# A hybrid attention and state-space layer: two token tiles to a PSUM bank, weights a job ahead, and the orders of TensorE and VectorE written by hand

## The chip, the cores and the metric

The kernel runs on one core of a Trainium2 chip. The core has a matrix engine (TensorE, PE in the profile), a vector engine (VectorE, DVE), an activation engine (ScalarE, ACT), a general engine (GpSimd, POOL) and a synchronisation engine (SyncE, SP). Each takes its own instructions strictly in order and waits at an instruction until its inputs and buffers are ready. SP and ACT also issue DMAs, in the place where these stand in their order. The metric is the device time of one execution in microseconds (us), given as the median of several runs.

## The reference

One layer over 1024 tokens of width 1024, in fp32, cut to what matters here:

```python
h = rmsnorm(x, g_pre)
q, k, v, g_att, z, xbc, dt_raw, merge_logits = split(h @ w_in)
# branch A: 8 heads, two softmax maps of 64 columns each, causal, with a bias by distance
a = softmax(q1 k1 / 8 + bias) - lam * softmax(q2 k2 / 8 + bias)
o = rmsnorm(a @ v, att_subln_g) * (1 - lambda_init) * silu(g_att)
y_att = o @ w_att_proj
# branch B: 8 groups of 4 heads of 64, state 128
xbc = silu(causal_conv4(xbc)); xs, B, C = split(xbc); dt = softplus(dt_raw + dt_bias)
y = chunked_scan(xs, dt, A, B, C) + xs * d_skip
y_ssm = group_rmsnorm(y * silu(z), ssm_norm_g) @ w_ssm_proj
mixed = sigmoid(gate_att) * y_att + sigmoid(gate_ssm) * y_ssm
out = x + rmsnorm(mixed @ w_out, g_post)
```

## The kernel before

Every fp32 operand of a projection is split into a rounded high part (made by ScalarE, helper `split`, L97) and a low part, the difference (VectorE or GpSimd, L98). A product is three matmuls, high x high, high x low and low x high (`mm3`, L153). A projection "step" with transposed output (`proj_T`) is 12 matmuls of 512 columns, half of a bank of 512 tokens; one with tokens on the partitions (`proj_N`) is 24 matmuls of 256 columns for one tile of 128 tokens.

The stages run one after the other:

- Start: x is loaded, scaled to h, transposed by TensorE (`ptx`) and split into hTH and hTL; keys, queries and values of head 0 are projected.
- Attention: for each of 8 heads, 8 blocks of 128 queries (`Block`, named by head and block). A block makes scores `s` on TensorE, adds the bias and takes the maximum on VectorE (`ng`), exponentials with their sums on ScalarE, and combines both maps on VectorE: `rec` (reciprocal of the sums), `nlam`, then `p`. While the next block begins, TensorE transposes `p` (`pta`), and multiplies it by the values (`po`). After four blocks `normed` computes the norm of the four outputs `o`: 11 small instructions (`rsv`, `rsy`, `rst`), then four products with the gate `gg`. Beside the blocks a stream of jobs, taken in steps (`stream.take`), projects keys (`pk`), queries (`pq`), values and gates (`pv`) of the next head, and the merge gates (`pg`).
- Attention projection (`pya`), then the state-space part: for each of 8 groups, convolutions of B, C and x (`pub`, `puc`, `pux`; evictions to `ub`, `bT` and so on, three taps, a tanh) and the gate z (`pz`), as jobs beside the 8 chunks of the group before. A chunk (`Chunk.prepare` and `advance`) loads decay rows by a DMA (`mt<-arow_d`), turns them into decays on ScalarE (L783), multiplies them by the masked product `cbm` on VectorE, and TensorE makes `pd` of it.
- Last group with the first half of the state-space projection (`pye`) beside it, then the rest of that projection (`pys`), the output projection (`pout`) and the final norm.

Accumulators come from three PSUM pools of two buffers each: `psp` (projections), `pss` (scores, and `pd`), `pst` (transposes, `po`, `px`). Weights come through buffers `raw`, three of them, issued on SP.

TensorE's order is the program's (`manual_schedule(engines={PE})`). The orders of the other engines are made by a scheduler, which goes by the program's order, its own estimates, and marks such as `tc.high_priority(offset=AHEAD)` around evictions.

Of the kernel before, what the change touches and what calls it, by code (L numbers as in the profile page):

```python
# [10 lines left out]
F32 = mybir.dt.float32  # L11
# [6 lines left out]
P = 128  # L18
# [28 lines left out]
AHEAD = 2000  # L47
# [27 lines left out]
def tile_hybrid_layer(ctx: ExitStack, tc: tile.TileContext, x, g_pre, w_in, lq1, lk1, lq2, lk2,  # L75
# [56 lines left out]
    def load_cols(w, row0, col0, width, tag, name, off=0, wh=None, wl=None, eng=None):  # L132

        if wh is None:
            wh = wts.tile([P, KT, width], F32R, tag=tag + "h", name=name + "h")
            wl = wts.tile([P, KT, width], F32R, tag=tag + "l", name=name + "l")
        for c in range(0, width - off, P):
            n = min(P, width - off - c)
            cols = slice(off + c, off + c + n)
            for k0 in range(0, KT, 4):  # L140
                raw = wts.tile([P, 4, P], F32, tag="raw", bufs=3, name=f"{name}r{off + c}_{k0}")
                r0 = row0 + k0 * P
                nc.sync.dma_start(raw[:, :, 0:n], w[r0:r0 + 4 * P, col0 + c:col0 + c + n].rearrange("(k p) c -> p k c", p=P))
                split(wh[:, k0:k0 + 4, cols], wl[:, k0:k0 + 4, cols], raw[:, :, 0:n], eng)
        return wh, wl
# [25 lines left out]
    def proj_N(w, t, n, name):  # L171

        wh, wl = w
        ps = psp.tile([P, 512], F32, tag="pp", name=name)
        sl = slice(t * P, (t + 1) * P)
        mm3(ps[:, 0:n], [((hTH[:, k, sl], hTL[:, k, sl]), (wh[:, k, 0:n], wl[:, k, 0:n])) for k in range(KT)])
        return ps

    class Stream:
# [5 lines left out]
        def add(self, load, steps):  # L185
            self.jobs.append([load, steps, None])

        def load(self, i):
            if i < len(self.jobs) and self.jobs[i][2] is None:
                self.jobs[i][2] = self.jobs[i][0]()  # L190

        def advance(self):

            if self.at is None:
                for i in range(self.ahead + 1):
                    self.load(self.done + i)
                self.at = self.jobs[self.done][1](self.jobs[self.done][2])
            try:
                next(self.at)
                return True  # L200
# [50 lines left out]
    pe_scope.enter_context(tc.manual_schedule(engines={mybir.EngineType.PE}))  # L251
# [10 lines left out]
    class Head:  # L262
# [15 lines left out]
        def keys(self, w, half):  # L278
# [3 lines left out]
            with tc.high_priority(offset=AHEAD):  # L282
                nc.scalar.activation(kh[lo, 0, sl], ps[lo], AF.Copy)
                nc.scalar.activation(kh[hi, 1, sl], ps[hi], AF.Copy)
                nc.vector.tensor_tensor(kl[lo, 0, sl], ps[lo], f32(kh[lo, 0, sl]), op=ALU.subtract)
                nc.vector.tensor_tensor(kl[hi, 1, sl], ps[hi], f32(kh[hi, 1, sl]), op=ALU.subtract)
            for part in (kh, kl):
                nc.scalar.dma_start(f32(part[hi, 0, sl]), f32(part[lo, 0, sl]))
                nc.scalar.dma_start(f32(part[lo, 1, sl]), f32(part[hi, 1, sl]))
            yield  # L290

        def queries(self, w, half):
# [3 lines left out]
            with tc.high_priority(offset=AHEAD):  # L296
                nc.scalar.activation(qs[lo, 0, sl], ps[lo], AF.Copy, scale=DK ** -0.5)
                nc.scalar.activation(qs[hi, 1, sl], ps[hi], AF.Copy, scale=DK ** -0.5)
                nc.vector.scalar_tensor_tensor(qs[hi, 0, sl], ps[lo], DK ** -0.5, f32(qs[lo, 0, sl]), op0=ALU.mult, op1=ALU.subtract)
                nc.vector.scalar_tensor_tensor(qs[lo, 1, sl], ps[hi], DK ** -0.5, f32(qs[hi, 1, sl]), op0=ALU.mult, op1=ALU.subtract)  # L300
            yield

        def load_values(self):
            wh = wts.tile([P, KT, 288], F32R, tag="wbh", bufs=1, name=f"wvh{self.h}")
            wl = wts.tile([P, KT, 288], F32R, tag="wbl", bufs=1, name=f"wvl{self.h}")
            load_cols(w_in, 0, OV + self.h * P, P, "", f"wv{self.h}", wh=wh, wl=wl, eng=nc.gpsimd)
            load_cols(w_in, 0, OG + self.h * P, 2 * P, "", f"wg{self.h}", off=P, wh=wh, wl=wl, eng=nc.gpsimd)
            return wh, wl

        def values(self, w):  # L310
            vv, gg = self.vv, self.gg
            for t in range(NT):
                ps = proj_N(w, t, 256, f"pv{self.h}_{t}")
                with tc.high_priority(offset=AHEAD):
                    nc.scalar.activation(vv[:, t, 0:DV], ps[:, 0:DV], AF.Copy)
                    nc.vector.tensor_tensor(vv[:, t, DV:], ps[:, 0:DV], f32(vv[:, t, 0:DV]), op=ALU.subtract)
                    nc.scalar.activation(gg[:, t, :], ps[:, DV:2 * DV], AF.Tanh, scale=0.5)
                    nc.vector.scalar_tensor_tensor(gg[:, t, :], gg[:, t, :], 1.0, ps[:, DV:2 * DV], op0=ALU.add, op1=ALU.mult)
                yield

# [6 lines left out]
    def load_wa(w, row0, col0, name):  # L327
        return lambda: load_cols(w, row0, col0, P, "wa", name, eng=nc.gpsimd)

    def add_head(head):  # L330
        h = head.h
        stream.add(load_wa(w_in, 0, OK + h * P, f"wk{h}"), both_halves(head.keys))
        stream.add(load_wa(w_in, 0, OQ + h * P, f"wq{h}"), both_halves(head.queries))
        stream.add(head.load_values, head.values)

    def add_gate(d):

        def steps(w, half):
            pg = yield from proj_T(w, half, f"pg{d}_{half}")
            th = wts.tile([P, 512], F32, tag="gt", name=f"gt{d}_{half}")  # L340
            with tc.high_priority(offset=AHEAD):
                nc.scalar.activation(th, pg, AF.Tanh, scale=0.5)
            nc.scalar.dma_start(sig_d[d, :, half * 512:half * 512 + 512], th)
            yield
        stream.add(load_wa(w_in, 0, OM + d * P, f"wm{d}"), both_halves(steps))

# [4 lines left out]
    with tc.tile_pool(name="norm", bufs=1, reuse_waits="tile") as work:  # L351
# [16 lines left out]
        first = [load_cols(w_in, 0, OK, P, "wa", "wk0", eng=nc.gpsimd), load_cols(w_in, 0, OQ, P, "wa", "wq0", eng=nc.gpsimd)]  # L368

        def scaled(half):  # L370
            ss = small.tile([P, 4], F32, tag="ss4", name=f"ssx{half}")
            for j in range(4):
                sq = work.tile([P, D], F32, tag="sq", bufs=1, name=f"sqx{half}_{j}")
                nc.scalar.activation(sq, xs[half * 4 + j], AF.Square, accum_out=ss[:, j:j + 1])
            r = rms(ss, 4, D, EPS, f"x{half}")
            for j in range(4):
                xt = xs[half * 4 + j]
                if j % 2:
                    nc.scalar.activation(xt, xt, AF.Copy, scale=r[:, j:j + 1])
                else:  # L380
                    nc.vector.tensor_scalar(xt, xt, r[:, j:j + 1], None, op0=ALU.mult)

        def turned(half, k):
            pt = pst.tile([P, 512], F32, tag="t", name=f"ptx{half}_{k}")
            for j in range(4):
                nc.tensor.transpose(pt[:, j * P:(j + 1) * P], xs[half * 4 + j][:, k * P:(k + 1) * P], ident)
# [5 lines left out]
        scaled(0)  # L392
        for k in range(KT):
            turned(0, k)
        with tc.high_priority(offset=AHEAD):
            scaled(1)
        keys, queries = head.keys(first[0], 0), head.queries(first[1], 0)
        next(keys)
        for run, ks in ((keys, (0, 1, 2)), (queries, (3, 4, 5)), (queries, (6, 7))):
            for k in ks:  # L400
                turned(1, k)
            next(run)
        for run in (keys, queries, head.keys(first[0], 1), head.queries(first[1], 1)):
            for _ in run:
                pass
        parameters(work)
        stream.add(head.load_values, head.values)
        head.load_near()

# [11 lines left out]
    class Block:  # L421
# [6 lines left out]
        def scores(self):  # L428
# [26 lines left out]
            sums = small.tile([P, 2, 2], F32, tag="sums", name=f"sums{nm}")  # L455
            for i, (s, l0, width) in enumerate(parts):
                for m in range(2):
                    nc.scalar.activation(self.p[i][:, m, 0:width], s[:, m, 0:width], AF.Exp, bias=neg[:, m:m + 1],  # L458
                                         accum_out=sums[:, i, m:m + 1])
            den = sums[:, 0, :]  # L460
            if len(parts) == 2:
                nc.vector.tensor_tensor(den, den, sums[:, 1, :], op=ALU.add)

            self.rec = small.tile([P, 2], F32, tag="rec", name=f"rec{nm}")
# [3 lines left out]
            for i, (_, _, width) in enumerate(parts):  # L468
# [3 lines left out]
        def weights(self):  # L472
            self.w = []
            for i, k0 in enumerate(range(0, self.qb + 1, 4)):
# [6 lines left out]
                with tc.high_priority(offset=200):  # L481
                    split(ah[:, 0:m, :], al[:, 0:m, :], pt[:, 0:m * P].rearrange("p (a b) -> p a b", b=P))
                self.w += [(ah[:, j, :], al[:, j, :]) for j in range(m)]

        def output(self):
            nm, qb, vv, rec = self.nm, self.qb, self.head.vv, self.rec
            po = pst.tile([P, 512], F32, tag="t", name=f"po{nm}")
            for k, (ah, al) in enumerate(self.w):
                nc.tensor.matmul(po[:, 0:256], ah, vv[:, k, :], start=(k == 0), stop=False)
                nc.tensor.matmul(po[:, 0:256], al, vv[:, k, :], start=False, stop=(k == qb))  # L490
            self.o = work.tile([P, DV], F32, tag="o", bufs=8, name=f"o{nm}")
            sq = work.tile([P, DV], F32, tag="sqo", bufs=2, name=f"sq{nm}")
            nc.scalar.activation(sq, po[:, DV:2 * DV], AF.Copy, scale=rec[:, 0:1])
            nc.vector.scalar_tensor_tensor(self.o, po[:, 0:DV], rec[:, 0:1], sq, op0=ALU.mult, op1=ALU.add)
            nc.scalar.activation(sq, self.o, AF.Square, accum_out=self.ss)

    def normed(head, part, blocks, ss):

        h = head.h
        r = rms(ss, 4, DV, EPS, f"o{h}_{part}")  # L500
        for j, b in enumerate(blocks):
# [12 lines left out]
    with tc.tile_pool(name="attn", bufs=2, reuse_waits="tile") as work:  # L514
        stream.finish(1)
        before = None
        softmax = [1.0 + 0.3 * qb + 0.4 * (qb >= 4) for qb in range(NT)]
        for h in range(HEADS):
            steps = 0
# [563 lines left out]
```

## Time and profile before

| what | value |
|---|---|
| time of 3 runs, median (lowest to highest) | 1950.76 us (1948.28 to 1950.99) |
| time of the profiled execution | 1953.8 us |
| its span | 1951.9 us |
| mean granted clock of TensorE | 0.978 |
| busy TensorE / VectorE / ScalarE / GpSimd | 1830.9 / 1159.9 / 858.7 / 473.6 us |
| instructions in the span | 27895 |

Busy time is the sum over an engine's instructions. An engine that is not busy waits, and the profile names what its next instruction waited for; the releaser is worked out from semaphore events. A line of the profile reads: line of the kernel, engine, operation, output <- inputs.

### The profile page before, as it was taken

The numbers are of one execution on the slowest core, as the hardware profiler recorded it, in microseconds if no ns is written. First come the engines' busy times: TensorE is split into PE (matmuls) and PEld (weight loads), VectorE is DVE, ScalarE is ACT, GpSimd is POOL, SyncE is SP. The second block draws the span as 40 slices with busy tenths as digits, with TensorE's granted clock in tenths as the row PEclk, the third lists the DMA queues.
The fourth block names the chain that finished last, engine by engine and source line by source line (L and its number), as shares of the span: only waits on it lengthen the run. The fifth ranks groups of instructions, "written<-read, shape, count | busy, mean of one in ns | idle before, by whom it ended". The sixth has DMA issues, their size and how long they took to land.

```text
span 1951.9 us, 27895 instructions
## 1 busy us (share of the span) xinstructions
PE 1830.9 (94%) x10249; PEld 1579.8 (81%) x10249; DVE 1159.9 (59%) x2564; ACT 858.7 (44%) x2143; POOL 473.6 (24%) x388
## 2 busy tenths in 40 slices
PE   4999999999999999999989899999999988798998
PEld 3888988889889888888778787888888876576886
DVE  4265665655656553126756759686867778564333
ACT  5345454555545443115544446455544455242211
POOL 2212111121111112212422314142332325341210
PEclk9999999999999999999999999999999998898999
DMA  5322122131221126422222223232322234674422
GB/s 164 87 55 79 36 82 58 49 84 39 73 63 44 58 73 208 150 75 63 65 55 76 65 72 91 55 91 56 82 61 74 75 95 152 206 239 132 157 83 79
DMA packets 225734, 175.64 MB, mean 90 GB/s; under 512 B 13116, under 2 KB 187550, under 8 KB 225598
## 3 DMA queue, kind: packets, MB, share of 16 engines
q1 hardware_dynamic: 193660, 116.48, 21.8%
q10 hardware_dynamic: 31938, 57.38, 8.8%
q8 instruction: 81, 1.33, 0.3%
q14 instruction: 55, 0.45, 0.1%
HBM read 133.82 MB, written 33.17 MB: 86 GB/s over the span
## 4 chain that ended last, share of the span: by engine, by line
PE 35%; DVE 8%; DMA 6%; ACT 3%; issue 2%; POOL 1%; SPq 0%; ACTq 0%; DVEq 0%; POOLq 0%
PE pys L153 6%; PE pz L153 6%; DMA mt<-arow_d 5%; PE pout L153 5%; PE puc L153 4%; PE pub L153 4%; PE pux L153 3%; DVE xT L728 3%; PE pd L793 2%; PE pg L153 1%; ACT mt L783 1%; PE pd L796 1%; PE pd L798 1%; DVE rst_y L107 1%; PE pye L153 1%
## 5 line engine op out<-in xcount | busy, mean ns | idle before, releaser
L153 PE MATMUL pz<-wzh,hTH 128*128 128x256 f32 (+1 forms) x512 | 157.2, 307 | 39.5 <-ACT xT L726 21.8
L153 PE MATMUL pz<-wzl,hTH 128*128 128x256 f32 (+1 forms) x512 | 151.4, 296 | 0.0
L153 PE MATMUL pz<-wzh,hTL 128*128 128x256 f32 (+1 forms) x512 | 150.8, 295 | 0.0
L783 ACT ACTIVATE mt<-mt,acs 128x128 f32<-128x128 f32 x256 | 86.5, 392 | 141.7 <-DMA mt<-arow_d 129.5
L153 PE MATMUL pv<-wvl,hTH 128*128 128x256 f32 x512 | 144.5, 282 | 0.0
L153 PE MATMUL pv<-wvh,hTL 128*128 128x256 f32 x512 | 144.2, 282 | 0.0
L153 PE MATMUL pv<-wvh,hTH 128*128 128x256 f32 x512 | 143.4, 280 | 0.0
L153 PEld LDWEIGHTS pz<-wzh,hTH 128*128 128x128 f32 x512 | 103.0, 201 | 46.3 <-ACT xT L726 24.9
L779 POOL TENSOR_TENSOR v<-xb,dsk 128x256 f32<-128x256 f32 x64 | 53.2, 831 | 225.7 <-ACT xb L768 205.1
L153 PEld LDWEIGHTS pz<-wzl,hTH 128*128 128x128 f32 x512 | 103.0, 201 | 0.4
L153 PEld LDWEIGHTS pz<-wzh,hTL 128*128 128x128 f32 x512 | 102.5, 200 | 0.0
L153 PEld LDWEIGHTS pv<-wvh,hTH 128*128 128x128 f32 x512 | 97.2, 190 | 0.6 <-PE pq L153 0.6
L153 PEld LDWEIGHTS pv<-wvl,hTH 128*128 128x128 f32 x512 | 96.7, 189 | 0.0
L153 PEld LDWEIGHTS pv<-wvh,hTL 128*128 128x128 f32 x512 | 96.1, 188 | 0.0
L447 DVE TENSOR_REDUCE ng<-s 128x2 f32<-128x1024 f32 (+2 forms) x96 | 91.5, 954 | 1.8
L728 DVE SCALAR_TENSOR_TENSOR xT<-ux,cw,xT 128x512 f32<-128x512 f32 x96 | 85.2, 887 | 11.8 <-ACT xT L726 11.0
L98 DVE TENSOR_TENSOR al<-pta,ah 128x512 fp32r<-128x512 f32 (+2 forms) x96 | 51.0, 554 | 50.1 <-ACT ah L97 49.0
L458 ACT ACTIVATE p<-s,ngm 128x512 f32<-128x512 f32 (+3 forms) x128 | 76.0, 611 | 7.0 <-DVE ngm L453 6.4
L805 POOL TENSOR_TENSOR st<-st,elast 128x256 f32<-128x256 f32 x48 | 39.1, 815 | 141.1 <-DVE st L806 113.3
L793 PEld LDWEIGHTS pd<-xdt,mt 128*128 128x128 f32 x512 | 65.5, 196 | 8.7 <-DVE mt L785 5.1
L490 PE MATMUL po<-vv,al 128*128 128x256 f32 x288 | 72.2, 284 | 0.0
L793 PE MATMUL pd<-xdt,mt 128*128 128x64 f32 x512 | 66.0, 273 | 6.0 <-DVE mt L785 6.0
(1110 smaller groups left out, 5697.7 us busy)
## 6 DMA issues: line engine op xcount, KB each, us to landing
mt<-arow_d SPq DMA_DIRECT2D x64, 256.0 KB, 5.0
sig_d<-gt ACTq DMA_DIRECT2D x32, 256.0 KB, 2.0
y_d<-yT ACTq DMA_DIRECT2D x32, 256.0 KB, 2.9
yT_l<-y_d SPq DMA_DIRECT2D x24, 256.0 KB, 4.9
kh<-kh ACTq DMA_DIRECT2D x32, 128.0 KB, 2.2
kl<-kl ACTq DMA_DIRECT2D x32, 128.0 KB, 2.6
o_d<-oT ACTq DMA_DIRECT2D x16, 256.0 KB, 2.0
oTl<-o_d SPq DMA_DIRECT2D x8, 512.0 KB, 4.3
```

The source lines that it names most:

```text
L98: (eng or nc.vector).tensor_tensor(l, src, f32(h), op=ALU.subtract)
L107: nc.vector.scalar_tensor_tensor(t, t, -0.5, v, op0=ALU.mult, op1=ALU.mult)
L153: nc.tensor.matmul(ps, a, b, start=(i == 0), stop=(i == n - 1))
L447: nc.vector.tensor_reduce(ng, s[:, :, 0:width], axis=AX.X, op=ALU.max, negate=True)
L458: nc.scalar.activation(self.p[i][:, m, 0:width], s[:, m, 0:width], AF.Exp, bias=neg[:, m:m + 1], accum_out=sums[:, i, m:m + 1])
L490: nc.tensor.matmul(po[:, 0:256], al, vv[:, k, :], start=False, stop=(k == qb))
L728: nc.vector.scalar_tensor_tensor(out_h, u[:, j:j + 512], cw3[:, j, ct:ct + 1], out_h, op0=ALU.mult, op1=ALU.add)
L779: nc.gpsimd.tensor_tensor(v4(self.v), xs, b4(dsk[:, hs]), op=ALU.mult)
L783: nc.scalar.activation(mt[:, i, :], mt[:, i, :], AF.Relu, scale=-1.0, bias=acs[:, c, g.g * HG + i:g.g * HG + i + 1])
L793: nc.tensor.matmul(pd[:, 0, i * PH:(i + 1) * PH], mt[:, i, :], self.xdt[:, i * PH:(i + 1) * PH], start=True, stop=True)
L796: nc.tensor.matmul(pd[:, 1, 256:512], self.xb[:, 256:384], self.xe, start=True, stop=True)
L805: nc.gpsimd.tensor_tensor(v4(new), v4(state), b4(elast[:, c, hs]), op=ALU.mult)
```

## The change

What it does:

- VectorE's order, too, becomes the program's (`ORDERED`), and all marks of priority go. To place work later than its text, `post(n, fn)` runs `fn` after `n` more steps of the stream; `tick()` counts a step and stands right behind it, so `post(1, ...)` runs at the end of the step that posts it.
- Attention: the combination is a method `combined()` of its own, called after `normed` and after 0.6 of the block's steps; `o` is one reduction over both halves of `po`, with the reciprocal left out of it and multiplied into the norm (four small instructions more in `normed`); values and gates are projected for two token tiles into one bank and evicted together, with low parts posted.
- Weights: four `raw` buffers; the jobs of all heads and groups are listed beforehand, so that loads run one job ahead also from head to head and from group to group; splits are posted two and three steps behind the load, on GpSimd.
- Start: squares of all eight x tiles first; the scaling of the second half stands behind the first half's transposes; transposes are written in pairs, some in `pss` banks; VectorE alone scales.
- State-space part: two tiles of z to a bank (except group 0); taps, tanh and gating of a convolution posted 1, 2 and 3 steps behind; `mt` issued on ScalarE's queue; its decays written ahead of `prepare`; the state's product on VectorE in place of GpSimd.
- Keys' copies between partitions (`kh<-kh`, `kl<-kl`) go from ScalarE's queue to SP's; so do the stores of `mix_d`. Projection and tail: loads of gates a job ahead, half of the `yT` loads on ScalarE's queue, the gated sum posted one step behind.

```diff
-AHEAD = 2000
+ORDERED = {getattr(mybir.EngineType, e) for e in ('PE', 'DVE')}
...
+    def post(n, fn):
+        item = [now[0] + n, fn]
+        posts.append(item)
+        return item
...
+    def tick():
+        now[0] += 1
+        for item in [i for i in posts if i[0] <= now[0]]:
+            run(item)
...
                 next(self.at)
+                tick()
                 return True
...
-    pe_scope.enter_context(tc.manual_schedule(engines={mybir.EngineType.PE}))
+    pe_scope.enter_context(tc.manual_schedule(engines=ORDERED))
...
+            nc.scalar.activation(qs[lo, 0, sl], ps[lo], AF.Copy, scale=DK ** -0.5)
+            nc.scalar.activation(qs[hi, 1, sl], ps[hi], AF.Copy, scale=DK ** -0.5)
+            def low():
                 nc.vector.scalar_tensor_tensor(qs[hi, 0, sl], ps[lo], DK ** -0.5, f32(qs[lo, 0, sl]), op0=ALU.mult, op1=ALU.subtract)
                 nc.vector.scalar_tensor_tensor(qs[lo, 1, sl], ps[hi], DK ** -0.5, f32(qs[hi, 1, sl]), op0=ALU.mult, op1=ALU.subtract)
+            post(1, low)
             yield
...
         r = rms(ss, 4, DV, EPS, f"o{h}_{part}")
+        for j, b in enumerate(blocks):
+            nc.vector.tensor_tensor(r[:, j:j + 1], r[:, j:j + 1], b.rec[:, 0:1], op=ALU.mult)
...
                     block.scores()
+                    if block.qb < 4:
+                        block.exponentials()
                     stream.take(0.05 * steps)
                     if before:
                         before.output()
-                        if j == 0:
-                            normed(*ended)
-                    stream.take(unit * softmax[block.qb])
+                    if block.qb >= 4:
+                        block.exponentials()
+                    if before and j == 0:
+                        normed(*ended)
+                    stream.take(unit * softmax[block.qb] * 0.6)
+                    block.combined()
+                    stream.take(unit * softmax[block.qb] * 0.4)
...
-            nc.sync.dma_start(self.mt, bass.AP(arow_d.tensor, arow_d.offset + self.group.g * HG * S + self.c * P,
+            nc.scalar.dma_start(self.mt, bass.AP(arow_d.tensor, arow_d.offset + self.group.g * HG * S + self.c * P,
...
+                    post(1, taps)
+                    post(2, lambda u=u, out_h=out_h: nc.scalar.activation(u[:, 0:512], out_h, AF.Tanh))
+                    post(3, gated)
```

The orders show what moves. First VectorE at the first block of head 4, before; `o_7`, `rsv_o`, `rst_o` and `rsy_o` belong to the norm of head 3's last four blocks, `rec`, `nlam` and `p` to the new block, and `kl` is the low part of head 5's keys:

```order
L465 RECIPROCAL rec_0_4408<-sums_0_4405 128x2
L467 SCALAR_TENSOR_TENSOR nlam_0_4410<-rec_0_4408,sums_0_4405,neg_lam 128x1
L470 SCALAR_TENSOR_TENSOR p_0_0_4404<-p_0_0_4404,nlam_0_4410 128x128
L494 SCALAR_TENSOR_TENSOR o_7_4463<-po_7_4446,rec_7_4300,sq_7_4464 128x128
L114 TENSOR_SCALAR rsv_o_1_4468<-sso_1_3794 128x4
```

The same place in the changed kernel, from the four small products to the combination (ahead of them stand the reduction `o_7` and the same 11 small instructions):

```order
L581 TENSOR_TENSOR rsy_o_1_4353<-rsy_o_1_4353,rec_4_3839 128x1
...
L581 TENSOR_TENSOR rsy_o_1_4353<-rsy_o_1_4353,rec_7_4251 128x1
L583 SCALAR_TENSOR_TENSOR o_4_3945<-o_4_3945,rsy_o_1_4353,gg_2457 128x128
...
L583 SCALAR_TENSOR_TENSOR o_7_4347<-o_7_4347,rsy_o_1_4353,gg_2457 128x128
L316 TENSOR_TENSOR kl_4277<-pk_0_4317,kh_4276 64x512
L317 TENSOR_TENSOR kl_4277<-pk_0_4317,kh_4276 64x512
L545 RECIPROCAL rec_0_4395<-sums_0_4308 128x2
L547 SCALAR_TENSOR_TENSOR nlam_0_4397<-rec_0_4395,sums_0_4308,neg_lam 128x1
L550 SCALAR_TENSOR_TENSOR p_0_0_4307<-p_0_0_4307,nlam_0_4397 128x128
```

The combination stood ahead of the norm and now stands behind it and behind `kl`; on TensorE the 12 matmuls of `pk` stand between `po` and `pta` in both kernels.

VectorE at the fourth block of head 4, before; `qs` is the low part of head 5's queries:

```order
L465 RECIPROCAL rec_3_4679<-sums_3_4676 128x2
L467 SCALAR_TENSOR_TENSOR nlam_3_4681<-rec_3_4679,sums_3_4676,neg_lam 128x1
L494 SCALAR_TENSOR_TENSOR o_2_4704<-po_2_4697,rec_2_4597,sq_2_4705 128x128
L470 SCALAR_TENSOR_TENSOR p_3_0_4675<-p_3_0_4675,nlam_3_4681 128x512
L299 SCALAR_TENSOR_TENSOR qs_4372<-pq_1_4684,qs_4372 64x512
L300 SCALAR_TENSOR_TENSOR qs_4372<-pq_1_4684,qs_4372 64x512
```

And in the changed kernel:

```order
L573 TENSOR_REDUCE o_2_4593<-po_2_4586 128x128
L332 SCALAR_TENSOR_TENSOR qs_4275<-pq_1_4569,qs_4275 64x512
L333 SCALAR_TENSOR_TENSOR qs_4275<-pq_1_4569,qs_4275 64x512
L545 RECIPROCAL rec_3_4613<-sums_3_4566 128x2
L547 SCALAR_TENSOR_TENSOR nlam_3_4615<-rec_3_4613,sums_3_4566,neg_lam 128x1
L550 SCALAR_TENSOR_TENSOR p_3_0_4565<-p_3_0_4565,nlam_3_4615 128x512
```

Both `qs` moved from behind `p` to ahead of `rec`; they read `pq`, whose last matmul stands just ahead of `pta` on TensorE.

Third, SP's queue in group 2 of the state-space part, before; the loads of `wx03r` and `wx13r` are weights of group 3:

```order
L143 DMA wx03r_0_11590<-in_w_in 128x4x128
L752 DMA mt_1_11226<-arow_d 128x4x128
L752 DMA mt_2_11362<-arow_d 128x4x128
L752 DMA mt_3_11461<-arow_d 128x4x128
L752 DMA mt_4_11565<-arow_d 128x4x128
L143 DMA wx03r_4_11594<-in_w_in 128x4x128
```

And ScalarE's in the changed kernel, around a chunk of group 4; L858 makes the decays, `sqy` is the square of a chunk's output, `sz` and `xb` evict PSUM banks:

```order
L795 ACTIVATE sz_12752<-pz_2_12840 128x512
L863 DMA mt_3_13108<-arow_d 128x4x128
L926 ACTIVATE sqy_7_12979,ssy_1_12296<-v_7_12744 128x256
L858 ACTIVATE mt_3_13108<-mt_3_13108,acs 128x128 x3
L795 ACTIVATE sz_12752<-pz_4_12913 128x512
L878 ACTIVATE xb_1_13007<-px_1_13002 128x512
```

The load of `mt` moved from SP's queue, between weights, to ScalarE's own, ahead of the decays by one row here.

601 lines of the change are left out of this document (347 added, 254 removed).

## The prediction

> **What bounds the kernel now.** I read the busy times by stage first, then what TensorE waited for, then the granted clock around those waits, and last the timeline of two attention blocks. First, busy time in six stretches of the span: each row gives the stretch and its length, then the busy time and instruction count of TensorE, of its weight loads, of VectorE, ScalarE and GpSimd, then granted clock, DMA share and GB/s. The stretches are the start, attention, the attention projection with the first z gate, the SSM groups, the last group with the first half of its projection, and the tail.
>
> ```profile
> 0.00:90.00 90.00, 61.49 (x355) 53.05 (x356) 32.60 (x71) 40.55 (x73) 15.44 (x16) 0.96 0.42 127
> 90.00:754.70 664.70, 657.28 (x4003) 577.58 (x4003) 400.21 (x1032) 334.06 (x973) 108.39 (x82) 1.00 0.24 69
> 754.70:928.00 173.30, 169.97 (x818) 143.32 (x817) 57.88 (x102) 45.18 (x89) 40.57 (x30) 0.99 0.35 104
> 928.00:1617.00 689.00, 645.53 (x3793) 567.29 (x3792) 498.16 (x1028) 344.28 (x815) 218.53 (x192) 0.98 0.27 72
> 1617.00:1709.00 92.00, 70.17 (x328) 56.21 (x326) 63.03 (x122) 35.26 (x81) 42.12 (x35) 0.87 0.61 188
> 1709.00:1951.90 242.90, 226.51 (x960) 182.37 (x960) 108.02 (x211) 59.40 (x116) 48.56 (x33) 0.96 0.42 137
> ```
>
> TensorE is the bound. Its order has the same matmuls in both kernels, rearranged only before attention, so the change can move the time only by TensorE's idle time and the clock behind it. Idle by stage (length less busy): start 28.5 us, attention 7.4, projection 3.3, SSM 43.5, last group 21.8, tail 16.4. Time lost to the clock, (1 - clock) x length: SSM 0.02 x 689 = 13.8 us, last group 12.0, tail 9.7, start 3.6. Attention is full and at full clock: there is little to win there, and all its 664.7 us can lose. The view of waits names what ends the idle times (total us, times, longest):
>
> ```profile
> PE pz L153 <- ACT xT L726: 21.8, 12, 4.0
> PE pz L153 <- DVE sz L707: 15.5, 12, 3.3
> PE ptx L386 <- DVE hTL L389: 14.5, 5, 7.1
> PE pys L153 <- ACT yT_h L97: 12.0, 1, 12.0
> PE ptx L386 <- DVE xt L381: 6.5, 1, 6.5
> PE pout L153 <- ACT mixH L1007: 6.2, 1, 6.2
> PE pta L480 <- DVE p L470: 3.0, 8, 0.6
> ```
>
> A wait costs more than its length. In the next rows (TensorE alone: stretch, length, busy and count, clock, DMA) a 2.7 us wait ends at 1491.1: behind it 18 matmuls take 3.9 us at clock 0.56, where 42 take 5.0 us at clock 1.00; 18 at that rate need 2.14 us, so the drop costs 1.76 us. The last row holds two waits of about 2 us without a drop.
>
> ```profile
> 1488.30:1491.10 2.80, 0.32 (x3) 1.00 0.25 94
> 1491.10:1495.00 3.90, 3.69 (x18) 0.56 0.00 0
> 1495.00:1500.00 5.00, 5.00 (x42) 1.00 0.55 139
> 983.00:990.00 7.00, 3.91 (x31) 1.00 0.15 37
> ```
>
> **Attention: what the written order of VectorE costs.** Before, a scheduler puts the softmax combination (rec, nlam, p) ahead of the rest; now it stands where the program calls combined(), behind normed() and behind the low parts that post(1) releases at the end of the same step. TensorE's transposes pta need p. The timeline at the first block of head 4 (start, duration):
>
> ```profile
> 413.63 0.28 PE L489 MATMUL po<-vv,ah 128*128 128x256 f32 x1
> 414.99 0.22 DVE L467 SCALAR_TENSOR_TENSOR nlam<-rec,sums,neg_lam 128x1 f32<-128x1 f32 x1
> 415.25 0.35 DVE L470 SCALAR_TENSOR_TENSOR p<-p,nlam 128x128 f32<-128x128 f32 x1
> 415.42 0.28 PE L490 MATMUL po<-vv,al 128*128 128x256 f32 x1
> 415.54 0.39 PE L153 MATMUL pk<-hTH,wk5h 128*128 128x512 f32 x1
> 416.96 0.17 DVE L114 TENSOR_SCALAR rsv_o<-sso 128x4 f32<-128x4 f32 x1 [0.47 <-ACT sq L495]
> 418.33 0.27 PE L480 MATMUL pta<-cst,p 128*128 128x128 f32 x1
> 419.14 1.14 DVE L502 SCALAR_TENSOR_TENSOR o<-o,rsy_o,gg 128x128 f32<-128x128 f32 x4
> 420.90 0.69 DVE L286 TENSOR_TENSOR kl<-pk,kh 64x512 fp32r<-64x512 f32 x1
> ```
>
> p was done at 415.6, 2.7 us before pta. The norm's chain runs from the last po at 415.42; TensorE covers it with one step of pk, 2.91 us to 418.33. In the new order the chain has to end first: po to rsv 1.54 with two evictions and a square, of which one eviction goes, say 1.25; the Newton steps 419.14 - 416.96 = 2.18; four new multiplies r x rec, at 0.2 each like those small steps, 0.8; the four o 1.14; two kl 1.4; rec and nlam 0.46; p 0.45 with its semaphore. That is 7.7 us against 2.9: a wait of 4.8. Six heads (1 to 6): 29 us. The last head has no kl: 3.4. Head 0 has kl but no norm: about 3. Sum 35 us. The work of ScalarE and TensorE that could cover it stands behind pta in their own queues.
>
> In the fourth block of a head the second half of pq ends just ahead of pta, and now both low parts of it (qs) stand ahead of rec, nlam and p:
>
> ```profile
> 439.31 0.17 DVE L465 RECIPROCAL rec<-sums 128x2 f32<-128x2 f32 x1 [1.57 <-ACT p L458]
> 439.90 0.74 DVE L470 SCALAR_TENSOR_TENSOR p<-p,nlam 128x512 f32<-128x512 f32 x1
> 440.28 0.40 PE L153 MATMUL pq<-hTH,wq5l 128*128 128x512 f32 x1
> 440.80 0.63 PE L480 MATMUL pta<-cst,p 128*128 128x128 f32 x4
> 441.66 0.59 ACT L298 ACTIVATE qs<-pq 64x512 fp32r<-64x512 f32 x1
> 442.99 0.69 DVE L300 SCALAR_TENSOR_TENSOR qs<-pq,qs 64x512 fp32r<-64x512 f32 x1
> ```
>
> From 440.28: the matmul 0.4, two evictions of 0.59, the second qs 0.69, rec 0.2, nlam 0.26, p 0.8: 3.6 us, where pta came 0.52 after: 3.1 us more, in seven heads 22 us.
>
> In the fifth block the norm's chain (1.25 + 2.18 + 0.8 + 1.14), vv and gg of two tiles (between 0.3 and 0.69 each, say 0.45), the sum, rec, nlam and p (1.45) make 7.7 us; TensorE covers it with two tiles of pv, 48 matmuls of 0.119 us (15 such steps from 413.63 to 415.42), 5.7 us. Wait 2, or up to 4 if the chain's square stands behind the block's four exponentials on ScalarE; I take 2.2, in seven heads 15, and 1 in the last. The seventh block has vv and gg of a pair ahead of p: 0.4 in seven heads, 3. Sum of new waits: 35 + 22 + 16 + 3 = 76 us; from the old 7.4 about 4 go. Fifteen waits (7 + 1 + 7) are 3 us or more. With 12 of them followed by a drop of 1.76 us: 21. **Attention: +93 us**, from +45 (waits a fifth shorter, none in the fifth block, no drops) to +125 (fifth block at 4, a drop at every wait).
>
> The Trainium skill ("TensorE: Matmul & The Clock Gate", Part 1) has the clock fall to half after one idle window of about 3.4 us. The trace here falls behind 2.7 us too. By the page alone the first and fourth blocks would fall fewer times, an estimated 7, and the sum would be 9 us lower.
>
> **The other parts.**
> - Start. Squares of all x tiles first, each half scaled by VectorE alone, transposes in pairs of banks, GpSimd splits the weights. The waits on hTL and xt, 21 us, came because the second half's scaling stood ahead of the first half's hTL; it now stands behind. The 6.1 us before the first load stay. I take -12, bounds -4 and -17.
> - Projection and first z gate: splits shared by two engines, gate loads a job ahead: 3.3 us idle; -3, bounds 0 and -4.
> - SSM. In the next rows (waits of ScalarE and of SP's queue in the SSM stage; then the landing of mt's DMA in one group) ScalarE waits 124 us for the decay rows mt, and behind it in its queue stand the evictions that TensorE's pz and pux wait for. SP issues mt between weight loads and waits 264 us for a free mt buffer.
>
> ```profile
> ACT mt L783 <- DMA mt<-arow_d: 123.6, 41, 7.0
> SPq L752 <- PE pd L793: 264.0, 38, 15.5
> DMA to landing us min/median/max: 4.8/5.3/5.8
> ```
>
> Now ScalarE issues mt itself, in its order only one to seven rows ahead of the first use, so it still waits up to 5.3 us per chunk, 64 times; what is new is that z evictions go two tiles to a bank, with half as many to be late, that taps and tanh are posted two ticks apart, and that VectorE has its order. Going through one group, an eviction held up by 5.3 us ends 0 to 4 us before its bank is wanted again: most of the waits go, one at the last pux stays. VectorE takes on GpSimd's product for the state and gives up half of its z instructions, so its 498 us stay within a few per cent, 72% of the stage. Of 43.5 + 13.8 = 57 us I take four fifths: -46, bounds -5 and -57.
> - Last group: 33.8 us idle or at low clock. The 12.0 us wait for yT_h ends a chain through the store of the last gate, which stays; half the loads go to ScalarE's queue. -12, bounds 0 and -20.
> - Tail: the order of eviction and second half puts mixH earlier; the 6.2 us wait with its drop of about 3 goes: -7, bounds 0 and -10.
>
> Sum of these: -80, bounds -45 and -105 (not all ends together). Net: +93 - 80 = **+13 us** on the profiled execution, 1953.8 us, which stands 3.0 above the median of the runs: 1967 profiled, 1964 as a median.
>
> **Rivals.**
> 1. Faster. The waits in attention stay at the low bound (+45) and the other parts reach their high one (-105): 1950.8 - 60 = 1891; halfway, 1915. For it: VectorE is idle for 40% of attention (400 of 665 us busy). Against: that idle time isn't at these places. It decides where the first block's wait is under 3 us. Chance 0.27.
> 2. ScalarE as mt's issuer. If its waits of 5.3 us at the head of its queue hold the evictions past their banks, the SSM stage gives 5 instead of 46: 1964 + 41 = 2005. For it: one to seven rows between issue and use; against: the 124 us of waiting are there already. It decides when a wait is longer than the 0 to 4 us of slack. Chance 0.2. The Trainium skill ("DMA: Bandwidth & Descriptors", Issuing engines are not separate DMA queues) says that another issuing engine saves only the time to issue; by that rule mt would land no sooner, which points to this rival. The 264 us that SP's queue stood still before issuing speak for more than that.
> 3. VectorE becomes the bound of the SSM stage: each written wait stops all behind it, and 498 of 689 us are busy already. At 5% over TensorE's 645 us: 678, a gain of 11 instead of 46: 1999. Chance 0.08.
> 4. Gains and losses cancel within the 4 us (0.2%) that a measurement of this kernel can't tell from nothing: 1947 to 1955. Chance 0.07.
>
> My forecast, attention +75 to +110 and the rest -60 to -95, has the remaining 0.38: 1955 to 1998 by itself. Faster (rival 1, and little beside it) 0.27, same 0.07, slower 0.66 (forecast, rivals 2 and 3). The range of 8 in 10 takes in the halfway point of rival 1 and rival 2 with a little: 1912 to 2008.
>
> **What would show it.** In the profile after: TensorE waits pta <- DVE p of some 76 us in all, near 4.8 in a head's first block and 3 in its fourth; granted clock in attention below 1.00, and the stage 750 us or more long; first scores at about 78 us; the SSM stage near 643 us with pz waits under 12 us; one wait of 8 to 10 us before the last projection. I would be wrong if pta's waits stay under 30 us, or if the SSM stage does not shrink.

## The result, and the profile after

The changed kernel takes 2022.33 us (median of 4 runs, 2019.32 to 2028.38) where the kernel before took 1950.88: ratio 1.0372, 95% interval 1.0346 to 1.0398. Its profiled execution took 2019.32 us with a span of 2017.4 us at a mean clock of 0.965. The direction was forecast, the size was not: +13 us on the profiled execution was expected, +65.5 came, past the upper end of the range.

Busy time by stage, first of the kernel after, in the columns of the first table of the prediction. The stages begin at the first `s`, `pya`, `pub`, `pye` and `pys`:

```profile
0.00:80.60 80.60, 59.88 (x355) 51.93 (x356) 30.39 (x67) 34.57 (x61) 15.48 (x16) 0.96 0.49 146
80.60:855.40 774.80, 682.18 (x4002) 599.09 (x4000) 418.81 (x1034) 310.12 (x852) 106.79 (x84) 0.96 0.20 57
855.40:982.00 126.60, 118.85 (x578) 100.10 (x578) 26.43 (x37) 21.90 (x38) 38.95 (x25) 0.96 0.41 130
982.00:1689.40 707.40, 685.03 (x4073) 604.25 (x4073) 558.62 (x1127) 375.83 (x854) 189.82 (x160) 0.99 0.29 76
1689.40:1777.80 88.40, 65.89 (x287) 51.84 (x285) 60.18 (x109) 33.33 (x69) 35.74 (x29) 0.86 0.61 194
1777.80:2017.40 239.60, 224.84 (x960) 183.18 (x960) 104.66 (x212) 57.80 (x112) 44.44 (x32) 0.96 0.43 135
```

The kernel before, cut at the same places (its start and attention rows are in the prediction; the prediction's projection row ran on to 928.0, but the stretch from 873.4 to there has no idle time of its own, so that both cuts hold the same 3.3 us of it):

```profile
754.70:873.40 118.70, 115.37 (x579) 99.18 (x577) 19.97 (x37) 18.65 (x36) 29.50 (x22) 0.99 0.41 123
873.40:1618.60 745.20, 700.84 (x4035) 611.95 (x4034) 537.67 (x1098) 372.10 (x869) 230.95 (x201) 0.98 0.27 71
1618.60:1709.50 90.90, 69.49 (x323) 55.73 (x323) 61.49 (x118) 34.47 (x79) 40.78 (x35) 0.87 0.62 192
1709.50:1951.90 242.40, 226.47 (x960) 182.33 (x960) 107.96 (x211) 58.90 (x115) 48.56 (x33) 0.96 0.42 136
```

| stage | forecast | measured |
|---|---|---|
| start | -12 | -9.4 |
| attention | +93 | +110.1 |
| projection and first z gate | -3 | +7.9 |
| state-space groups | -46 | -37.8 |
| last group | -12 | -2.5 |
| tail | -7 | -2.8 |
| sum | +13 | +65.5 |

Attention's 110 us are 85.2 of idle time (774.80 - 682.18 = 92.6, before 7.4) and 24.9 of matmuls that run longer at the lower clock. TensorE's waits in the whole kernel after:

```profile
PE pta L560 <- DVE p L550: 86.6, 37, 4.5
PE pys L180 <- ACT yT_h L97: 11.1, 2, 10.8
PE pd L910 <- DVE st L917: 11.1, 6, 2.8
PE pd L905 <- DVE xdt L893: 7.5, 3, 5.8
PE ptx L447 <- DVE xt L430: 7.3, 4, 6.8
PE pye L180 <- ACT we5h L97: 4.8, 1, 4.8
```

The waits of pz, 37.3 us before, are gone from the head of the list; pta's, 3.0 us before, lead it. The timeline shows how each comes about. First block of head 4, from the last matmuls of po to pta:

```profile
465.10 0.28 PE L569 MATMUL po<-vv,al 128*128 128x256 f32 x1
466.40 0.17 DVE L114 TENSOR_SCALAR rsv_o<-sso 128x4 f32<-128x4 f32 x1 [0.56 <-ACT sq L574]
468.58 0.37 DVE L581 TENSOR_TENSOR rsy_o<-rsy_o,rec 128x1 f32<-128x1 f32 x4
468.87 1.14 DVE L583 SCALAR_TENSOR_TENSOR o<-o,rsy_o,gg 128x128 f32<-128x128 f32 x4
470.62 0.69 DVE L317 TENSOR_TENSOR kl<-pk,kh 64x512 fp32r<-64x512 f32 x1
471.80 0.35 DVE L550 SCALAR_TENSOR_TENSOR p<-p,nlam 128x128 f32<-128x128 f32 x1
472.30 0.45 PE L560 MATMUL pta<-cst,p 128*128 128x128 f32 x1 [4.17 <-DVE p L550]
```

This is the chain of the prediction, 7.2 us in place of 7.7: the four small multiplies overlap and take 0.37 us together, not 0.8. Fourth block:

```profile
496.20 0.63 ACT L97 ACTIVATE wk6h<-wk6r 128x512 fp32r<-128x512 f32 x1 [0.81 <-issue]
497.33 0.59 ACT L329 ACTIVATE qs<-pq 64x512 fp32r<-64x512 f32 x1
497.95 0.68 DVE L332 SCALAR_TENSOR_TENSOR qs<-pq,qs 64x512 fp32r<-64x512 f32 x1 [3.89 <-ACT qs L329]
498.65 0.69 DVE L333 SCALAR_TENSOR_TENSOR qs<-pq,qs 64x512 fp32r<-64x512 f32 x1
499.56 0.37 DVE L547 SCALAR_TENSOR_TENSOR nlam<-rec,sums,neg_lam 128x1 f32<-128x1 f32 x1
500.86 0.52 PE L560 MATMUL pta<-cst,p 128*128 128x128 f32 x2 [4.51 <-DVE p L550]
```

VectorE starts the first qs only behind ScalarE's second eviction (497.33 + 0.59), so both low parts, 1.4 us, lie on the path, not one; ahead of the evictions ScalarE splits a weight, 0.63 us, so that they start 0.4 us behind the last matmul of pq. Seventh block, where GpSimd splits the next head's value weights:

```profile
538.79 2.51 POOL L98 TENSOR_TENSOR wvl<-wv6r,wvh 128x512 fp32r<-128x512 f32 x2 [38.88 <-ACT wvh L97]
538.89 1.20 DVE L542 TENSOR_TENSOR sums<-sums 128x2 f32<-128x2 f32 x1
540.13 0.17 DVE L545 RECIPROCAL rec<-sums 128x2 f32<-128x2 f32 x1
540.33 0.98 DVE L547 SCALAR_TENSOR_TENSOR nlam<-rec,sums,neg_lam 128x1 f32<-128x1 f32 x1
542.25 0.94 PE L560 MATMUL pta<-cst,p 128*128 128x128 f32 x6 [2.03 <-DVE p L550]
```

An addition of two numbers a row takes 1.20 us beside GpSimd. This is so in heads 0 to 5. In head 6, which has no values left to prepare, GpSimd splits nothing at this place: the addition takes 0.15 us, and pta waits 0.22. The fifth block waits less than forecast, and the first block of the last head, which has no kl, 2.75 us:

```profile
515.07 0.30 PE L560 MATMUL pta<-cst,p 128*128 128x128 f32 x1 [1.10 <-DVE p L550]
...
755.92 0.30 PE L560 MATMUL pta<-cst,p 128*128 128x128 f32 x1 [2.75 <-DVE p L550]
```

### The profile page after: what moved, and what is told of

It is laid out like the page before. It is cut to its first block, busy times and chain, and to the rows that moved or that the text cites. A ratio compares the mean times of both kernels' runs of the same rounds, so it can differ in the third digit from the quotient of the medians.

```text
span 2017.4 us, 27792 instructions
## 1 busy us (share of the span) xinstructions
PE 1836.7 (91%) x10249; PEld 1590.4 (79%) x10249; DVE 1199.1 (59%) x2584; ACT 833.5 (41%) x1983; POOL 431.2 (21%) x344
## 4 chain that ended last, share of the span: by engine, by line
PE 24%; DVE 15%; DMA 7%; ACT 4%; issue 2%; POOL 1%; SPq 0%; ACTq 0%; DVEq 0%; POOLq 0%
PE pz L180 6%; PE pys L180 4%; PE pout L180 4%; DVE xT L820 3%; DMA mt<-arow_d 3%; PE pub L180 2%; DVE cT L820 2%; PE puc L180 1%; PE pd L905 1%; PE pg L180 1%; PE pux L180 1%; DMA yT_l<-y_d 1%; DVE mt L892 1%; DVE rsy_y L108 1%; PE pye L180 1%
## 5 line engine op out<-in xcount | busy, mean ns | idle before, releaser
L180 PE MATMUL pz<-wzh,hTH 128*128 128x256 f32 (+1 forms) x512 | 150.2, 293 | 5.7 <-DVE sz L798 2.9
L180 PE MATMUL pz<-wzl,hTH 128*128 128x256 f32 (+1 forms) x512 | 146.1, 285 | 0.0
L180 PE MATMUL pz<-wzh,hTL 128*128 128x256 f32 (+1 forms) x512 | 145.3, 284 | 0.0
L560 PE MATMUL pta<-cst,p 128*128 128x128 f32 x288 | 48.7, 293 | 90.1 <-DVE p L550 86.6
L858 ACT ACTIVATE mt<-mt,acs 128x128 f32<-128x128 f32 x256 | 86.8, 392 | 93.8 <-DMA mt<-arow_d 88.8
L560 PEld LDWEIGHTS pta<-cst,p 128*128 128x128 f32 x288 | 33.8, 146 | 107.6 <-issue 90.4
L180 PEld LDWEIGHTS pz<-wzh,hTH 128*128 128x128 f32 x512 | 97.6, 191 | 7.0 <-issue 3.1
L180 PEld LDWEIGHTS pz<-wzl,hTH 128*128 128x128 f32 x512 | 97.4, 190 | 0.5
L180 PEld LDWEIGHTS pz<-wzh,hTL 128*128 128x128 f32 x512 | 97.0, 189 | 0.0
L97 ACT ACTIVATE ah<-pta 128x512 fp32r<-128x512 f32 (+2 forms) x96 | 44.7, 490 | 107.8 <-PE pta L560 105.9
L573 DVE TENSOR_REDUCE o<-po 128x128 f32<-128x256 f32 x64 | 27.1, 423 | 96.0 <-PE po L569 95.8
```

Of the source, the lines that this page charges most:

```text
L97: nc.scalar.activation(h, src, AF.Copy)
L180: nc.tensor.matmul(ps, a, b, start=(i == 0), stop=(i == n - 1))
L560: nc.tensor.transpose(pt[:, j * P:(j + 1) * P], self.p[i][:, 0, j * P:(j + 1) * P], ident)
L573: nc.vector.tensor_reduce(self.o, po[:, 0:2 * DV].rearrange("p (t c) -> p c t", t=2), axis=AX.X, op=ALU.add)
L858: nc.scalar.activation(mt[:, i, :], mt[:, i, :], AF.Relu, scale=-1.0, bias=acs[:, c, g.g * HG + i:g.g * HG + i + 1])
```

## The experiments

All ratios are to the kernel before, run on the same chip; the chips differ from run to run, and the kernel before took 1946 to 1951 us on them. The first three take VectorE's order in attention apart.

**p ahead of all.** In the block loop:

```diff
+                    block.combined()
                     if before and j == 0:
                         normed(*ended)
                     stream.take(unit * softmax[block.qb] * 0.6)
-                    block.combined()
```

> The changed kernel with one call moved: block.combined() stands ahead of normed() and of the steps, in every block, so that rec, nlam and p come before the norm and before the posted low parts in VectorE's order. Theory (VectorE's written order in attention puts p too late): the waits pta <- DVE p, 86.6 us, fall under 10 us, the granted clock of attention returns to 1.00 and the stage from 774.8 to about 668 us: the whole 2022 to about 1915 us (1905 to 1930). Rival (ScalarE's order without priorities, or the copies of keys on SP's queue, hold attention up): the time stays above 1990 us.

Measured: 1916.58 us, ratio 0.9839 (0.9821 to 0.9856). Attention, by stage and by waits:

```profile
79.80:742.20 662.40, 652.13 (x4002) 577.79 (x4000) 408.34 (x1034) 308.92 (x852) 107.80 (x84) 1.00 0.23 66
PE pta L560 <- DVE p L550: 3.0, 14, 0.3
```

One moved call gives back all that attention lost, idle time and clock alike, and turns the change into a gain. The rival falls: ScalarE's order has no priorities here either, and the copies are on SP's queue still. (The scheduler lets ScalarE's order follow VectorE's a little: in the fifth block of head 3 a square stands between the exponentials, where it stood behind them.)

**Only the norm behind p.** `normed(*ended)` moved behind `block.combined()`, which stays behind the first 0.6 of the steps.

> The changed kernel with only normed() moved behind combined(); the low parts of keys, queries, values and gates stay ahead of p. Theory: the first block of a head waits for kl alone, 2.9 us in place of 4.2, the fifth block (1.1 us) no longer; fourth and seventh stay at 4.5 and 2.0. The waits pta <- DVE p fall from 86.6 to about 68 us, and the time from 2022 to about 2002 us (1995 to 2010). Rival (the norm is the whole of the loss): below 1960 us.

Measured: 2011.26 us, ratio 1.0323 (1.0305 to 1.0342).

```profile
80.80:841.80 761.00, 682.09 (x4002) 598.83 (x4000) 418.19 (x1035) 310.13 (x852) 106.81 (x84) 0.96 0.20 58
PE pta L560 <- DVE p L550: 50.0, 22, 4.5
PE pta L560 <- DVE rsv_o L114: 22.0, 6, 3.7
```

Attention falls by 13.8 us only: in the first block kl takes over (the six waits of the second line, up to 3.7 us where 2.9 was expected; their releaser is named rsv_o, the instruction behind p), and fourth and seventh stay. It is not the whole loss, and at 11 us of time not the 20 expected.

**Only the low parts behind p.** `post(1, low)` becomes `post(2, low)` for keys, queries, values.

> The changed kernel with the low parts of keys, queries, values and gates posted two steps behind in place of one, so that they stand behind p; normed() stays ahead of it. Theory: the fourth and the seventh block's waits (4.5 and 2.0 us, seven heads each) go, the first block waits for the norm alone, 2.8 us in place of 4.2, the fifth stays near 1.1: the waits fall from 86.6 to about 28 us, some eight clock drops go too, and the time falls from 2022 to about 1950 us (1940 to 1962). Rival (the norm is the loss, the low parts are hidden anyway): above 2000 us.

Measured: 1956.82 us, ratio 1.0041 (1.0023 to 1.0059).

```profile
81.10:785.70 704.60, 663.50 (x4002) 587.90 (x4000) 411.29 (x1034) 310.76 (x852) 107.68 (x84) 0.98 0.22 63
PE pta L560 <- DVE p L550: 35.1, 22, 2.8
```

Attention falls by 70.2 us, the first block's wait to 2.8 as expected. The waits sum to 35.1 us, not 28: two steps later the second low parts of the queries stand ahead of the fifth block's norm, and its wait grows from 1.1 to 1.86. The low parts were the larger share. Both edits alone give 84 of 112 us; the rest needs both, since norm and kl cover each other in the first block.

**Value weights split by VectorE.** The changed kernel with `eng=nc.vector` in both loads of `load_values`.

> The changed kernel with the weights of values and gates (wv, wg) split by VectorE in place of GpSimd; in VectorE's order these splits stand elsewhere than ahead of p in the seventh block. Theory (the seventh block's wait is 2.0 us and not 0.4 because VectorE's small instructions are stretched while GpSimd splits these weights: 1.20 us for one of 0.16): the wait falls to about 0.5 us in seven heads, the sum of pta's waits from 86.6 to about 76, unless a new wait for the splits appears elsewhere. Rival (the wait comes from VectorE's own order): 2.0 us stays.

Measured: 2027.99 us, ratio 1.0417 (1.0398 to 1.0436). Seventh block of head 4, and fourth:

```profile
541.50 0.15 DVE L542 TENSOR_TENSOR sums<-sums 128x2 f32<-128x2 f32 x1
543.04 0.41 PE L560 MATMUL pta<-cst,p 128*128 128x128 f32 x2 [0.22 <-DVE p L550]
...
502.84 1.09 PE L560 MATMUL pta<-cst,p 128*128 128x128 f32 x4 [6.08 <-DVE p L550]
```

Without GpSimd beside it the addition takes 0.15 us and the wait falls from 2.03 to 0.22: the stretching was the cause. The splits, now in VectorE's queue, lengthen the fourth block's wait from 4.5 to between 5.5 and 6.8 and the first's from 4.2 to between 4.8 and 6.2, so the sum of pta's waits stays (88.8 us).

**Decay rows on SP's queue again.** `nc.sync.dma_start(self.mt, ...)` in the changed kernel.

> The changed kernel with the load of the decay rows mt issued on SP again; the rest of the change stays. Theory (mt's place on SP's queue behind weight loads caused the waits of the state-space groups before): the stage, 707 us after the change and 745 before, goes back to about 735 us and the time to about 2050 us. Rival (the written order, the pairs of z tiles and the posted taps took the waits away, with weights a job ahead SP's queue is clear): within 8 us of 2022 us.

Measured: 2062.54 us, ratio 1.0585 (1.0558 to 1.0611). The state-space stage, and what ScalarE waited for there, then the same wait in the changed kernel:

```profile
982.70:1735.60 752.90, 705.15 (x4073) 616.90 (x4072) 551.63 (x1126) 373.65 (x853) 186.81 (x159) 0.97 0.27 71
ACT mt L858 <- DMA mt<-arow_d: 125.6, 40, 6.8
```

```profile
ACT mt L858 <- DMA mt<-arow_d: 81.4, 39, 5.2
```

The stage is 45.5 us longer, the time 2.1%: the move of mt carries the gain, and without it the stage is 8 us longer than in the kernel before.

**Only that move, in the kernel before.** One line, `nc.sync` to `nc.scalar` for mt.

> The kernel before with one line changed: the decay rows mt are loaded from ScalarE's queue; VectorE's order, tiles, posts and weights are those of before. Theory (mt's place on SP's queue was the cause of the waits in the state-space groups): the stage falls from 745 us by 20 to 40, the time to 1910 to 1930 us. Rival (mt's place pays only beside weights a job ahead and the posted taps; alone the wait for the landing moves to ScalarE's queue): within 8 us of before, or slower.

Measured: 1936.55 us, ratio 0.9926 (0.9902 to 0.9949). The stage falls from 745.2 to 731.2 us: less than the 20 to 40 of the theory, and more than the rival's nothing. The move pays three times as much beside the rest of the change.

**The state's product on GpSimd again**, with p ahead of all; in `Chunk.advance`:

```diff
-                    nc.vector.tensor_tensor(v4(new), v4(state), b4(elast[:, c, hs]), op=ALU.mult)
+                    nc.gpsimd.tensor_tensor(v4(new), v4(state), b4(elast[:, c, hs]), op=ALU.mult)
```

> The kernel with combined() first (1916 us), with the product of the state back on GpSimd. Theory (VectorE's queue is what pd <- st waits for, 11.1 us in six waits): with one instruction of 0.42 us less a chunk on VectorE the waits fall to about 5 us, the time by 4 to 8 us. Rival (GpSimd's 0.8 us product and the slower VectorE beside it cost as much): no change or up to 10 us slower.

Measured: 1895.59 us, ratio 0.9719 (0.9696 to 0.9741), 1.2% below the kernel with p ahead of all. That one's stage and wait, then this one's:

```profile
868.90:1584.70 715.80, 693.56 (x4072) 610.62 (x4072) 558.85 (x1128) 376.21 (x855) 189.38 (x160) 0.98 0.29 75
PE pd L910 <- DVE st L917: 11.1, 6, 2.7
```

```profile
869.60:1567.80 698.20, 685.56 (x4073) 605.69 (x4072) 546.05 (x1085) 376.13 (x855) 213.29 (x204) 0.99 0.30 77
PE pd L910 <- DVE st L917: 3.1, 3, 1.9
```

The waits fall by 8 us, more than forecast, and matmuls run 8.0 us shorter (693.56 to 685.56) at the higher clock. The stage is 17.6 us shorter. It took 707 to 716 us in the seven kernels here that share its code and 697 to 698 in the three with the product on GpSimd, so that 9 to 19 us are the product's; the time's 1.2% is beyond both intervals. This part of the change was a loss.

**One token tile to a bank again**, for values and z, in the kernel just named.

> The kernel with combined() first and the product of the state on GpSimd (1895.6 us), with one token tile to a bank again for values (pv) and for z (pz). Theory (a pair halves the evictions and leaves more time for each, while ScalarE stands up to 5.3 us at the landing of mt): waits of pz come back in the state-space stage, 698 us by the two-tile kernel, and the time is 6 to 20 us longer; attention stays at 662 us, since p stands ahead of vv and gg. Rival (the pairs do nothing, the posts and mt's own queue removed the waits): within 3 us of 1895.6.

Measured: 1950.36 us, ratio 1.0013 (0.9997 to 1.0029), 55 us above it. Its state-space stage and the longest waits there:

```profile
878.40:1625.50 747.10, 700.75 (x4073) 615.97 (x4072) 551.60 (x1116) 379.26 (x883) 213.92 (x204) 0.97 0.27 72
PE pz L180 <- DVE sz L796: 15.0, 7, 6.0
PE pz L180 <- ACT xT L812: 13.3, 5, 3.3
```

The pairs are worth 49 us in this stage, and 7.5 in attention (669.9 against 662.4), where none was expected; that is three to nine times what I gave them. A reading that no run here tests: with orders written out, an eviction comes when its turn comes, and a bank that holds two tiles gives it twice the time; a pair also halves the number of evictions, and the two were not taken apart. Pairs and mt's queue are each needed for the gain.

**Projection.** Two edits on kernels with p ahead of all: splits of its inputs by VectorE alone, and (with the state on GpSimd) the second and third weights loaded from ScalarE's queue, so that the loads of o come earlier on SP's, with three splits written ahead of the next gate step.

> The kernel with combined() first (1916 us), with one more edit: in the attention projection all splits of its inputs are made by VectorE, none by GpSimd. Theory (GpSimd's slow splits, pya <- oTl 3.5 us in 4 waits, make the stage 126.7 us long where it was 118.7): the stage falls to about 122 us and the time by 3 to 6 us. Rival (the stage is longer because the last head's output comes late and all splits stand right ahead of their use, whoever makes them): within 2 us of 1916, or slower.

> The kernel with combined() first and the product of the state on GpSimd (1895.6 us); in the attention projection the weights of the second and third job are loaded from ScalarE's queue in place of SP's, so that on SP the eight loads of o come right behind the first weights, and three splits of o stand ahead of the next gate step. Theory (the stage is 8 us longer than before because the loads of o stand on SP's queue behind weights that wait for raw buffers): the stage falls from 126.7 to about 120 us, the time by 4 to 8 us. Rival (ScalarE makes the high parts only behind the last gates, and its order, not the loads, sets the start): the stage stays within 2 us.

Measured: 1911.23 us, ratio 0.9800 (0.9778 to 0.9823), the stage 125.8 us; and 1895.06 us, ratio 0.9735 (0.9717 to 0.9753), the stage 128 us. Neither edit shortens the stage as its theory had it. The first's time is some 5 us lower, the theory's size, but only 0.9 us of that lies in the stage, and the intervals touch: inconclusive. The second falls: its first load of o starts on SP at 719.86, 12.8 us earlier than in the kernel that it builds on (732.66), yet the high parts start at 741.25 where they started at 741.82, behind a weight split that ScalarE sat 4.53 us for and the last gate:

```profile
719.86 21.29 SPq L650 DMA_DIRECT2D oTl<-o_d  x8
739.72 0.63 ACT L97 ACTIVATE wpa1h<-wpa1r 128x512 fp32r<-128x512 f32 x1 [4.53 <-PE pg L180]
740.26 0.58 ACT L384 ACTIVATE gt<-pg 128x512 f32<-128x512 f32 x1
741.25 5.83 ACT L97 ACTIVATE oTh<-oTl 128x1024 fp32r<-128x1024 f32 x6
```

So earlier loads do not help, and ScalarE's order puts these splits behind the last gate, as the rival had it; that moving them would shorten the stage was not tried.

**w_out spread** over the chunks 2 to 7 of the last group, with p ahead of all.

> The kernel with combined() first (1916 us), with the loads of w_out spread over the chunks 2 to 7 of the last group in place of pairs in the chunks 4 to 7. Theory (the weights of pye stand behind w_out's loads on SP's queue, pye <- we5h and we6h 6.8 us): these waits go, the last group falls from 90 to about 84 us, the time by 4 to 8 us. Rival (SP's queue or the raw buffers hold some weights up in any order): the wait moves to another pye, within 2 us of 1916.

Measured: 1912.03 us, ratio 0.9807 (0.9784 to 0.9830), which overlaps that of the kernel with p ahead of all; the group goes from 90.6 to 87.0 us, and one wait of 10.5 us for we6h stands where two of 3.3 and 3.5 stood. Inconclusive: the time is 4.6 us lower, near the low end of the theory, but the wait moved, as the rival had it.

**Three edits together**: p ahead of all, state on GpSimd, with the VectorE splits and w_out spread.

> The kernel with combined() first and the product of the state on GpSimd (1895.6 us), with the two small edits as well: projection splits by VectorE and the loads of w_out spread. Theory (the edits lie in different stages and add up): 3 to 10 us less, 1886 to 1893 us. Rival (the small edits gave nothing of their own, since the projection stage moved by 0.9 us and a wait of 10.5 us took the place of those removed): 1894 to 1898 us.

Measured: 1891.01 us, ratio 0.9705 (0.9683 to 0.9726): the fastest here, 56 us below the kernel before on its chip and 131 below the changed one. The time lies in the theory's range, but against the kernel with the first two edits the intervals overlap, so the small edits are not told from nothing.

## Why the prediction was right or wrong

- The bound and the mechanism were right: TensorE's instructions are the same, pta waits for p as VectorE's written order says, and p ahead of all takes the whole loss away. pta's waits were forecast at 76 us and measured 86.6, longer matmuls at 21 and measured 24.9.
- Sizes within attention, 17.1 us of the 52.5 by which the sum was short: the first block 4.2 us (4.8 forecast). The fourth, mis-sized most: 4.5 us (3.1); the term "the second qs 0.69" counted one low part where the row of before (its second qs at 442.99 and 0.69 long) already had two in series. The seventh 2.0 us in six heads (0.4): I took durations from instructions that had VectorE alone. The fifth 1.1 (2.2). By the granted clock a drop follows each of the 15 waits of 2.7 us or more, where 12 were counted on, and attention's mean fell to 0.96.
- By the Trainium skill ("TensorE: Matmul & The Clock Gate", Part 1), with its idle window of about 3.4 us, there would have been fewer drops: here the clock fell behind the last head's wait of 2.75 us too. The 2.7 us from the trace came nearer, but it is no sharp bound. Behind the six waits of 2.0 us in the seventh blocks the clock fell once (0.51 over 3.4 us in head 0, 1.00 in heads 1 and 2); in the run with only the low parts behind p it fell behind six of seven waits of 2.74 us and two of seven of 1.86. What else decides is open.
- The step that failed is the sum of the other parts: -80 forecast, -44.6 measured, the edge of its own bounds and 35.4 us of the 52.5. Of its terms only the product of the state was taken out by a run; the others are read from waits.
  - The projection (-3, measured +7.9, outside its bounds), where pya waits 7.2 us for the splits of o that two engines were to speed up (it waited for none before); they stand behind ScalarE's last gate.
  - The state-space stage (-46, measured -37.8), where the product of the state on VectorE, costed at "a few per cent" of busy time, lost 9 to 19 us, since VectorE's share rose to 558.62 of 707.40 us, 79%, and its queue is what pd waits for.
  - The last group (-12, measured -2.5), where the wait for yT_h fell from 12.0 to 10.8 us only, and new waits for we5h and we6h, 6.7 us, took the place of old ones.
  - The tail (-7, measured -2.8), where mixH's wait fell from 6.2 to 2.6 us and one of 2.7 for the last weight came.
- Rival 2, mt on ScalarE's queue as a loss, was wrong: its waits there fell to 81.4 us, and putting mt back costs 2.1%. The rule of the Trainium skill ("DMA: Bandwidth & Descriptors", Issuing engines are not separate DMA queues), that another issuing engine saves only the time to issue, holds for the transfer: once issued, mt lands no faster (median 5.1 us in the state-space stage, 5.0 before). Taken as a sign of rival 2 it misled. With mt on SP again, where mt and the weights wait in order behind one another (217.1 us ahead of mt's own issue), ScalarE waits 125.6 us for its landing in place of 81.4. SP's queue as a whole stands still about as long either way, 695 us and 665 without mt; what each of the waits in it costs was not taken apart. Rival 3 was right in kind and small in size.
- The range failed because its upper end took rival 2 alone and not the high end of attention's forecast, +110, together with the low bound of the rest, -45; both came.

## What to carry to other kernels

When an order is written by hand, put first on each engine what the bottleneck engine waits for next, and post everything else behind it; one call in the wrong place cost 112 us of attention here, and the profile shows it as waits of the bottleneck for one line. Take the parts of a large change apart even when its sum is a loss: two parts of this one were worth some 40 and 55 us, and a third lost about 20. When costing a chain from a trace, count every instruction that is serial there, and look at what runs beside it on GpSimd.

## What the runs showed of the hardware that was not expected

VectorE's smallest instructions took 1.20 and 0.98 us while GpSimd ran splits of 128 x 512, where they take 0.16 and 0.22 alone; moving the splits off GpSimd brought 0.15 us back. They were held rather than slowed: GpSimd's two splits ran from 538.79 to 540.08 and from 540.03 to 541.29, the addition ended at 540.09 and nlam at 541.31, as the splits did, and it is so in all six heads. The reciprocal between them, which reads one input where the two others combine two, started at 540.13 beside the second split and took its usual 0.17 us. Two instructions on one or two numbers a row so made 1.8 us of a wait of TensorE's. That the number of inputs decides is a reading of these three instructions; no run varied it.
